# Token-major projection blocks 512 columns wide on two PSUM banks, in a two-layer hybrid encoder

## The chip, the cores and the metric

One core of one Trainium2 chip runs the whole program. The metric is the device time of one execution in microseconds (us). A profiled execution is a separate one; its span runs from the first to the last profiled instruction.

## The reference

Input x is (1, 256, 2048) in float32. After a LayerNorm come two layers, each with an input projection of 6144 columns, an SSM over half of the width (64 groups of 16 channels, 64 states, both directions), differential attention with 8 heads over the other half, and an output projection with a residual and a LayerNorm:

```python
x = layer_norm(x, ln_emb_g, ln_emb_b)
for l in range(DEPTH):                                  # 2
    u, g_ssm, q, k, v, g_attn = split(x @ w_in[l])      # 1024 columns each
    y = u * ssm_d[l] + s5_scan(u, forward) + s5_scan(u, backward)
    y = gelu(y); y = y * sigmoid(y @ w_glu[l] + b_glu[l])
    y_ssm = y * silu(g_ssm)
    o = (softmax(q1 k1') - lam * softmax(q2 k2')) @ v   # 8 heads, q and k rotated
    y_attn = rms_norm(o) * attn_norm_g[l] * (1 - lambda_init) * silu(g_attn)
    x = layer_norm(ALPHA * x + concat(y_ssm, y_attn) @ w_out[l])
```

## The kernel before

All weights are streamed once, in jobs of 512 KB that a list `jobs` (lines 124 to 139) orders for both layers: `load` (143) brings a job into one of four `raw` buffers on SP's DMA queue, six jobs ahead of its use, and `do_split` (155) casts it, two jobs ahead, into a high part `wh` (ScalarE, line 162) and a low part `wl` (VectorE, line 164). A product is three matmuls, high by high, high by low, low by high (`mm3`, 167 to 170). Activations stand in x pairs `xh0`, `xl0` (the first 1024 rows of the contraction) and `xh1`, `xl1`, laid out with the 256 tokens in the free dimension.

A job holds 4 contraction tiles of 128 by 256 columns, so it is 24 matmuls of 256 columns (`sub_step`, 841). Where `tok_major` is false the weights are the stationary operand and the 256 tokens move: q, k, u, both gates, the GLU. Where it is true 128 tokens are stationary and 256 weight columns move: v and the output projection. A `block` (859) is 4 jobs into one PSUM bank of the tag `acc`, which has two banks; blocks alternate between them. The output projection's blocks are 2 jobs for each half of its contraction: first the attention half (line 943, result with the residual in `part_r`), after the GLU the SSM half (976), whose last blocks run token half by token half (988 to 1014) so that the LayerNorm of the first half begins early.

Beside the jobs run helpers ("lanes", 754 to 798): after each job `step` (829) calls `side`, which lets helpers of priority below 2 take a step and gives the others 1.6 us of VectorE cost (`BUDGET`). A helper says with each step what it costs and how many jobs it wants to wait. `ssm_load` (403) brings in B and C and transposes them, `ssm_in` (460) and `ssm_scan` (544) run the states, `ssm_out` (557) makes y by way of DRAM and, in `split_y` (621), its Gelu and its split. `head` (699) is one attention head: scores, softmax, product with v, RMS norm, and, after a further hop, two transposes of `on` into `oT` (746 to 750). `rotary_split` (690) prepares q and k. For the second layer `ssm_load` is started in the last stage of the first (971 to 979): it loads the tables and B there and the rest in the second layer's first jobs.

Instructions get their place on their engine by a list scheduler that works with estimated times; each engine then runs its list in order. `after` (115) keeps an instruction behind a given one of the same engine. `ln_finish` (214) ends a layer; in the last one it cuts the second token half's columns into pieces (`LAST_PIECES`, in units of 128) and stores each with two DMAs from SP (line 240).

Of the kernel before, what the change touches and what calls it, by code (L numbers as in the profile page):

```python
# [20 lines left out]
KT = 4  # L21
# [10 lines left out]
LAST_PIECES = (6,5,5)  # L32
# [7 lines left out]
HEAD_HOPS = (1,1,2,2,2,3)  # L40


@with_exitstack
def kernel(
# [80 lines left out]
    for l in range(DEPTH):  # L125
        for s in range(4):
            jobs += [(l, "in", 0, s), (l, "in", 1, s)]
        order = [2, 3]
        for hp in range(4):
            order += [8 + hp, 12 + hp, 16 + hp]  # L130
        order += list(range(20, 24)) + list(range(4, 8))
        for cb in order:
            jobs += [(l, "in", cb, s) for s in range(4)]
        for cb in range(8):
            jobs += [(l, "out", cb, 2), (l, "out", cb, 3)]
        for cb in range(4):
            jobs += [(l, "glu", cb, 0), (l, "glu", cb, 1)]
        for cb in range(8):
            jobs += [(l, "out", cb, 0), (l, "out", cb, 1)]
    raws, split = {}, {}  # L140
    newest = [None]

    def load(i):
        if i >= len(jobs):
            return
        l, kind, cb, s = jobs[i]
        src = {"in": w_in, "glu": w_glu, "out": w_out}[kind][l]
        raw = T([128, KT, 256], "raw", RAW_BUFS)
        newest[0] = SY.dma_start(
            raw,  # L150
            src[s * KT * 128:(s + 1) * KT * 128, cb * 256:(cb + 1) * 256].rearrange("(k p) c -> p k c", p=128),
# [3 lines left out]
    def do_split(i, wh=None, wl=None, behind=None):  # L155
# [3 lines left out]
        if wh is None:  # L159
            wh = T([128, KT, 256], "wh", SPLIT_AHEAD + 1, F32R)  # L160
            wl = T([128, KT, 256], "wl", SPLIT_AHEAD + 1, F32R)
        A.copy(wh, raw)  # L162
        with after(behind):
            V.tensor_tensor(wl, raw, wh.bitcast(F32), sub)  # L164
        split[i] = (wh, wl)

    def mm3(o, lh, ll, rh, rl, first, last):
        PE.matmul(o, lhsT=lh, rhs=rh, start=first, stop=False, skip_group_check=True)  # L168
        PE.matmul(o, lhsT=lh, rhs=rl, start=False, stop=False, skip_group_check=True)  # L169
        PE.matmul(o, lhsT=ll, rhs=rh, start=False, stop=last, skip_group_check=True)  # L170
# [43 lines left out]
    def ln_finish(r, gt, bt, st, dst, box, ahead):  # L214
# [16 lines left out]
        def norm(i, k0, nk, mv, rstd):  # L231
# [63 lines left out]
    def ssm_tables():  # L295
# [65 lines left out]
        for l in range(2):  # L361
# [3 lines left out]
            else:  # L365
                tt = [T([128, 2, 256], "v", 2) for _ in range(2)] + [T([128, 1, 256], "on")]
# [190 lines left out]
    def ssm_out(l):  # L557
# [74 lines left out]
        for o in range(9):  # L632
# [13 lines left out]
            if o < 8:  # L646
                part(ws[o], z, o, 2, z.C, 1, 0, sub, 1)
                toep(o)
                yield 1.8, 0, 0.5
        load_y()  # L650
        yield 0.0, 2
# [47 lines left out]
    def head(hp, h, q, k, v, oT, neg, gsc):  # L699
# [33 lines left out]
        for i in range(2):  # L733
            for k in range(2):
                PE.matmul(o[:, i, :], lhsT=wT[:, k, i * 128:(i + 1) * 128], rhs=v[:, k, h * 128:(h + 1) * 128],  # L735
                          start=k == 0, stop=k == 1)
        ms = T([128, 2], "ms", 2)
        on = T([128, 2, 128], "on")
# [119 lines left out]

    def block(hi, lo, n=4, tok_major=False):
# [5 lines left out]
    for l in range(DEPTH):  # L865
# [6 lines left out]
        else:  # L872
            l_tab = l_load = Lane(l_load, 1)
# [28 lines left out]
        oT = T([128, 8, 256], "a8", 3)  # L902
        store = {}
        heads, every = [], []
        for hp in range(4):
# [15 lines left out]
            every += [Lane(head(hp, h, store["q"], store["k"], v, oT, neg, gsc), 1 + 0.1 * h) for h in range(2)]  # L921
            heads = every[-2:]
        for b in range(4):
            acc = block(hi, lo)
            if b == 3:
                for a in every:
                    finish(a)
            sg = T([128, 2, 256], "qs" if b == 3 else "sh")
            A.activation(sg, acc, AF.Silu)
            V.tensor_tensor(oT[:, 2 * b:2 * b + 2, :], oT[:, 2 * b:2 * b + 2, :], sg, mult)  # L930
        sgs = T([128, 8, 256], "a8", 3)
        for b in range(4):
            acc = block(hi, lo)
            A.activation(sgs[:, 2 * b:2 * b + 2, :], acc, AF.Silu)

        M = Pair()
        for c in range(4):
            cs = slice(2 * c, 2 * c + 2)
            A.copy(M.h[0][:, cs], oT[:, cs])
            V.tensor_tensor(M.l[0][:, cs], oT[:, cs], M.h[0][:, cs].bitcast(F32), sub)  # L940

        part_r = [T([128, D], tag) for tag in ("xh1", "xl1")]
        for cb in range(8):
            cs = slice(cb * 256, (cb + 1) * 256)
            xr = T([128, 2, 256], "xr", 2)
            SY.dma_start(xr, xres[:, cs].rearrange("(i p) d -> p i d", p=128))
            acc = acc_bank()
            for s in (0, 1):
                sub_step(acc, s, M.hi, M.lo, 0, 7, tok_major=True)
# [21 lines left out]
        if l + 1 < DEPTH:  # L971
            l_load = ssm_load(l + 1)
# [104 lines left out]
```

## Time and profile before

| | us |
|---|---|
| median of 3 runs | 1000.04 (999.7 to 1003.74) |
| profiled execution | 1002.55 |
| its span | 1000.8 |

In the profile PE is TensorE's matmuls, PEld its weight loads, DVE is VectorE, ACT ScalarE, POOL GpSimd, SP the engine whose queue issues the DMAs. Matmuls overlap one another, so a matmul's duration is not what it costs; the distance between starts is. The granted clock of a stretch is the mean share of TensorE's full clock of 2.4 GHz, and 1.2 GHz is its other level. Times of single instructions are from the span's start. The first layer's jobs run to about 505 us, the second's from about 517.

### The profile page before, as it was taken

The numbers are of one execution on the slowest core, as the hardware profiler recorded it, in microseconds if no ns is written. First come the engines' busy times: TensorE is split into PE (matmuls) and PEld (weight loads), VectorE is DVE, ScalarE is ACT, GpSimd is POOL, SyncE is SP. The second block draws the span as 40 slices with busy tenths as digits, with TensorE's granted clock in tenths as the row PEclk, the third lists the DMA queues.
The fourth block names the chain that finished last, engine by engine and source line by source line (L and its number), as shares of the span: only waits on it lengthen the run. The fifth ranks groups of instructions, "written<-read, shape, count | busy, mean of one in ns | idle before, by whom it ended". The sixth has DMA issues, their size and how long they took to land.

```text
span 1000.8 us, 24625 instructions
## 1 busy us (share of the span) xinstructions
PE 955.8 (96%) x10304; PEld 926.8 (93%) x10304; DVE 780.3 (78%) x1353; ACT 576.0 (58%) x950; POOL 71.7 (7%) x103
## 2 busy tenths in 40 slices
PE   2999999999999998999979999999999999999995
PEld 2989988999999998999979989999999999999995
DVE  6875799899887786656588699899899759565676
ACT  2546588565575697545344585555556769843640
POOL 1000130210200000000011030010100100000001
PEclk9999999999999999999989999999999999999998
DMA  9898521545554643779875724555445454576953
GB/s 272 254 256 230 184 81 44 168 149 169 156 183 153 193 145 104 234 228 260 215 231 167 233 68 126 170 169 161 157 150 187 151 168 136 178 237 209 270 173 85
DMA packets 193167, 177.76 MB, mean 178 GB/s; under 512 B 37536, under 2 KB 185760, under 8 KB 193056
## 3 DMA queue, kind: packets, MB, share of 16 engines
q1 hardware_dynamic: 193056, 176.18, 58.7%
q8 instruction: 81, 1.33, 0.6%
q14 instruction: 30, 0.25, 0.1%
HBM read 165.02 MB, written 11.14 MB: 176 GB/s over the span
## 4 chain that ended last, share of the span: by engine, by line
PE 81%; DMA 7%; DVE 6%; ACT 3%; issue 1%; SPq 1%; POOL 0%; POOLq 0%; DVEq 0%; ACTq 0%
PE acc L168 23%; PE acc L169 23%; PE acc L170 23%; DMA raw<-in_w_out_dram 3%; PE ss L596 2%; DVE wl L164 2%; PE ss L501 1%; PE sc L707 1%; PE ss L735 1%; PE tp L473 1%; ACT wh L162 1%; PE tp L577 1%; DVE w L456 1%; DVE H L235 1%; DMA H<-in_x_dram 1%
## 5 line engine op out<-in xcount | busy, mean ns | idle before, releaser
L164 DVE TENSOR_TENSOR wl<-raw,wh 128x1024 fp32r<-128x1024 f32 x266 | 324.9, 1223 | 143.0 <-ACT wh L162 141.8
L162 ACT CAST wh<-raw 128x1024 fp32r<-128x1024 f32 x266 | 278.2, 1050 | 251.0 <-PE acc L169 118.7
L168 PE MATMUL acc<-xh,wh 128*128 128x256 f32 x1280 | 370.9, 290 | 0.8 <-ACT xh L252 0.5
L169 PE MATMUL acc<-xl,wh 128*128 128x256 f32 x1280 | 365.2, 286 | 0.8 <-DVE xl L253 0.7
L170 PE MATMUL acc<-xh,wl 128*128 128x256 f32 x1280 | 364.1, 285 | 1.1 <-DVE wl L164 1.1
L168 PEld LDWEIGHTS acc<-xh,wh 128*128 128x128 f32 x1280 | 245.5, 192 | 6.2 <-ACT xh L252 1.4
L169 PEld LDWEIGHTS acc<-xl,wh 128*128 128x128 f32 x1280 | 245.7, 192 | 2.4 <-DVE xl L253 1.5
L170 PEld LDWEIGHTS acc<-xh,wl 128*128 128x128 f32 x1280 | 245.6, 192 | 2.1 <-DVE wl L164 1.5
L168 PE MATMUL acc<-wh,xh 128*128 128x256 f32 x512 | 146.3, 286 | 0.0
L169 PE MATMUL acc<-wl,xh 128*128 128x256 f32 x512 | 145.4, 284 | 0.0
L170 PE MATMUL acc<-wh,xl 128*128 128x256 f32 x512 | 145.0, 283 | 0.0
L169 PEld LDWEIGHTS acc<-wl,xh 128*128 128x128 f32 x512 | 98.2, 192 | 0.2
L168 PEld LDWEIGHTS acc<-wh,xh 128*128 128x128 f32 x512 | 98.1, 192 | 0.1
L170 PEld LDWEIGHTS acc<-wh,xl 128*128 128x128 f32 x512 | 98.2, 192 | 0.0
L169 PE MATMUL acc<-wl,a 128*128 128x256 f32 x208 | 59.1, 286 | 2.1 <-DVE wl L164 2.1
L168 PE MATMUL acc<-wh,a 128*128 128x256 f32 x208 | 58.7, 284 | 0.0
L170 PE MATMUL acc<-wh,a 128*128 128x256 f32 x208 | 58.5, 283 | 0.0
L551 DVE TENSOR_TENSOR sa<-tab,H 128x256 f32<-128x256 f32 x126 | 53.0, 421 | 2.9 <-ACT H L504 0.7
L458 DVE TENSOR_TENSOR w<-w,x 128x512 f32<-128x512 f32 x64 | 45.6, 712 | 0.8
L169 PEld LDWEIGHTS acc<-wl,a 128*128 128x128 f32 x208 | 39.7, 191 | 3.3 <-DVE wl L164 3.3
L717 ACT ACTIVATE e<-sc,mx 128x256 f32<-128x256 f32 x64 | 29.5, 477 | 21.0 <-DVE mx L711 21.0
L168 PEld LDWEIGHTS acc<-wh,a 128*128 128x128 f32 x208 | 39.7, 191 | 0.4 <-ACT wh L162 0.4
(198 smaller groups left out, 1482.9 us busy)
## 6 DMA issues: line engine op xcount, KB each, us to landing
raw<-in_w_in_dram SPq DMA_DIRECT2D x192, 512.0 KB, 3.8
raw<-in_w_out_dram SPq DMA_DIRECT2D x64, 512.0 KB, 4.6
raw<-in_w_glu_dram SPq DMA_DIRECT2D x16, 512.0 KB, 4.4
xr<-xres SPq DMA_DIRECT2D x16, 256.0 KB, 4.3
xres<-H SPq DMA_DIRECT2D x14, 256.0 KB, 3.4
H<-in_x_dram SPq DMA_DIRECT2D x8, 256.0 KB, 5.9
u_dr<-ub SPq DMA_DIRECT2D x8, 256.0 KB, 3.3
a<-u_dr SPq DMA_DIRECT2D x8, 256.0 KB, 3.8
```

The costliest lines, as they stand in the source:

```text
L162: A.copy(wh, raw)
L164: V.tensor_tensor(wl, raw, wh.bitcast(F32), sub)
L168: PE.matmul(o, lhsT=lh, rhs=rh, start=first, stop=False, skip_group_check=True)
L169: PE.matmul(o, lhsT=lh, rhs=rl, start=False, stop=False, skip_group_check=True)
L170: PE.matmul(o, lhsT=ll, rhs=rh, start=False, stop=last, skip_group_check=True)
L235: last = V.scalar_tensor_tensor(r[:, i, cs], r[:, i, cs], rstd, bt[:, cs], mult, add)
L456: V.tensor_tensor(dst, t.unsqueeze(2).to_broadcast([128, 8, 16, 4]), M[:, m, gs, :].unsqueeze(3).to_broadcast([128, 8, 16, 4]), mult)
L458: V.tensor_tensor(w[:, r], w[:, r], x2, op)
L473: PE.transpose(t[:, pr, :], ws[o][:, ri, 2 * pr:2 * pr + 2].rearrange("p g c j -> p (g c j)"), ident)
L551: V.tensor_tensor(a.rearrange("p v q r g -> p v q (r g)"), lam, h.unsqueeze(1).to_broadcast([128, 2, 16, 8]), mult)
L596: PE.matmul(yps[d][halves[g2], pr, :], lhsT=w[halves[d], ri, g].rearrange("p c j -> p (c j)"), rhs=h[:, ::-1] if d else h, start=ri == 0, ...
L717: A.activation(e[:, m, i, :], sc[:, m, i, :], AF.Exp, bias=mx[:, c:c + 1], accum_out=sm[:, c:c + 1])
```

## The change

Blocks of v, of the attention gate and of the output projection become wide: a job of theirs is 2 contraction tiles by 512 columns, of the same 512 KB, with 128 tokens stationary, and a block fills both `acc` banks, one for each token half. v is done for four heads at a time. The attention half of the output projection is four wide blocks of 4 jobs; of the SSM half three wide blocks in the first layer and two in the second, the rest as before. A head leaves its result in `oh` with tokens in rows; the gate is applied there, and `to_mix` transposes and splits it inside the last SSM-gate block. The residual comes in two tiles per block. k's rotary is finished at once. The Gelu is kept behind the newest weight cast; y's load and split are a helper of their own. In the second layer all of `ssm_load` runs in the first jobs, with its tables' and B's DMAs behind the newest raw load. The last LayerNorm's pieces are 6, 5, 3, 2, and of each pair of output stores the second is issued by ScalarE.

```diff
-LAST_PIECES = (6,5,5)
+LAST_PIECES = (6,5,3,2)
+WIDE = (3, 2)
+Y_HOP = 3
+LATER_HOP = 2
...
+        for n in range(2):
+            order += [("in", 8 + 2 * n), ("inw", 8 + n), ("in", 12 + 2 * n), ("in", 9 + 2 * n), ("in", 13 + 2 * n)]
+        order += [("inw", 10), ("inw", 11)] + [("in", cb) for cb in range(4, 8)]
...
+        return (2, 512) if jobs[i][1] in ("inw", "wide") else (KT, 256)
...
-        A.copy(wh, raw)
+        newest[2] = A.copy(wh, raw).ins
...
-                for j in range(2):
-                    SY.dma_start(dst[2 * i + j][:, cs], r[64 * j:64 * j + 64, i, cs])
+                for j, eng in enumerate((SY, A)):
+                    eng.dma_start(dst[2 * i + j][:, cs], r[64 * j:64 * j + 64, i, cs])
...
-            SY.dma_start(tabs[l], tab_dr)
+            with after(newest[0]):
+                SY.dma_start(tabs[l], tab_dr)
+            yield 0.0, LATER_HOP
...
-            SY.dma_start(nat[64 * ri:64 * ri + 64], src[l].rearrange("d g p c -> g d (p c)"))
-            yield 0.0, 1 + ri
+            with after(newest[0] if l else None):
+                SY.dma_start(nat[64 * ri:64 * ri + 64], src[l].rearrange("d g p c -> g d (p c)"))
+            yield 0.0, 1 + ri * (4 if l else 1)
...
-                A.activation(z.yT[:, cs], z.yT[:, cs], AF.Gelu_apprx_tanh)
+                with after(newest[2]):
+                    A.activation(z.yT[:, cs], z.yT[:, cs], AF.Gelu_apprx_tanh)
...
+    def ssm_y(l):
+        load_y, split_y = ssm[l].y_lane
         load_y()
-        yield 0.0, 2
+        yield 0.0, Y_HOP
         split_y()
...
-        yield 0.0, HEAD_HOPS[4]
-        t = tp_bank([128, 256])
-        for i in range(2):
-            PE.transpose(t[:, i * 128:(i + 1) * 128], on[:, i, :], ident)
-        A.activation(oT[:, 2 * hp + h, :], t, AF.Copy, scale=gsc)
...
+    def wide_block(hi, lo, s0, n):
+
+        accs = [PS([128, 512], "acc", 2) for _ in range(2)]
+        for s in range(s0, s0 + n):
+            def fn(wh, wl):
+                for i in range(2):
+                    ms = slice(128 * i, 128 * i + 128)
+                    for k in range(2):
+                        kt = 2 * s + k
+                        mm3(accs[i], hi(kt)[:, ms], lo(kt)[:, ms], wh[:, k, :], wl[:, k, :],
+                            kt == 2 * s0, kt == 2 * (s0 + n) - 1)
+            step(fn)
+        return accs
...
-            l_tab = l_load = Lane(l_load, 1)
+            l_tab = l_load = Lane(ssm_load(l), 1)
...
+            if hp % 2 == 0:
+                accs = wide_block(hi, lo, 0, 8)
+                finish(rq)
+                v = T([128, 2, 512], "v")
+                for i in range(2):
+                    A.copy(v[:, i], accs[i])
...
-            rk.one()
-            acc = block(hi, lo, tok_major=True)
-            v = T([128, 2, 256], "v", 2)
-            A.copy(v, acc)
             finish(rk)
...
+        def to_mix(b):
+
+            for c in range(2 * b, 2 * b + 2):
+                t = tp_bank([128, 2, 256])
+                for n in range(2):
+                    for i in range(2):
+                        with after(newest[3]):
+                            PE.transpose(t[:, n, 128 * i:128 * i + 128],
+                                         oh[:, i, (2 * c + n) * 128:(2 * c + n + 1) * 128], ident)
+                cs = slice(2 * c, 2 * c + 2)
+                A.activation(M.h[0][:, cs], t, AF.Copy, scale=gsc)
+                V.scalar_tensor_tensor(M.l[0][:, cs], t, gsc, M.h[0][:, cs].bitcast(F32), mult, sub)
+
+        for b in range(2):
+            accs = wide_block(hi, lo, 0, 8)
+            for a in every[4 * b:4 * b + 4]:
+                finish(a)
+            cs = slice(512 * b, 512 * b + 512)
+            for i in range(2):
+                sg = T([128, 512], "qs" if i else "sh")
+                A.activation(sg, accs[i], AF.Silu)
+                V.tensor_tensor(oh[:, i, cs], oh[:, i, cs], sg, mult)
...
+            for n in range(4):
+                sub_step(acc, n, hi, lo, 0, 15)
+                if b == 3 and n in (1, 2):
+                    to_mix(n - 1)
...
+        for cb in range(4):
+            cs = slice(cb * 512, (cb + 1) * 512)
+            xrs = []
             for i in range(2):
-                V.scalar_tensor_tensor(part_r[i][:, cs], xr[:, i], ALPHA, acc[:, i, :], mult, add)
-        finish(l_out)
+                xrs.append(T([128, 512], "xr", 2))
+                SY.dma_start(xrs[i], xres[128 * i:128 * i + 128, cs])
+            accs = wide_block(M.hi, M.lo, 0, 4)
+            for i in range(2):
+                V.scalar_tensor_tensor(part_r[i][:, cs], xrs[i], ALPHA, accs[i], mult, add)
+        finish(l_y)
...
-        if l + 1 < DEPTH:
-            l_load = ssm_load(l + 1)
...
+        for cb in range(WIDE[l]):
+            accs = wide_block(M.hi, M.lo, 4, 4)
+            cs = slice(cb * 512, (cb + 1) * 512)
+            for i in range(2):
+                V.tensor_tensor(r[:, i, cs], part_r[i][:, cs], accs[i], add)
+                for c in range(2):
+                    ln_stats(r, i, 2 * cb + c, st)
+        for cb in range(2 * WIDE[l], late[0]):
```

## Rows read from the trace of the kernel before

**Rows 1.** Page, part 1: busy us, share of the span, instructions, by engine
```profile
PE 955.8 (96%) x10304; PEld 926.8 (93%) x10304; DVE 780.3 (78%) x1353; ACT 576.0 (58%) x950; POOL 71.7 (7%) x103
```

**Rows 2.** Page, part 4: the chain that ended last, by engine
```profile
PE 81%; DMA 7%; DVE 6%; ACT 3%; issue 1%; SPq 1%; POOL 0%; POOLq 0%; DVEq 0%; ACTq 0%
```

**Rows 3.** Stretches: length; busy PE, PEld, DVE, ACT, POOL; granted clock, DMA share, GB/s
```profile
380.00:392.00 12.00, 9.15 (x203) 8.69 (x200) 8.40 (x14) 10.44 (x19) 0.00 (x0) 0.87 0.37 112
470.00:505.00 35.00, 33.11 (x264) 31.74 (x263) 21.86 (x35) 13.42 (x13) 0.00 (x0) 1.00 0.89 219
505.00:530.00 25.00, 20.15 (x150) 19.21 (x149) 21.75 (x39) 8.59 (x14) 2.54 (x4) 0.86 0.69 216
614.00:770.00 156.00, 156.00 (x1334) 153.86 (x1334) 141.66 (x290) 87.78 (x175) 11.32 (x18) 1.00 0.53 163
877.00:922.00 45.00, 45.00 (x378) 45.00 (x377) 27.32 (x33) 16.45 (x16) 0.00 (x0) 1.00 0.75 232
```

**Rows 4.** Timeline of TensorE: start, us, engine, line, op, out<-in, shapes, count
```profile
172.79 1.05 PE L735 MATMUL ss<-v,wT 128*128 128x128 f32 x8
...
454.83 0.28 PE L168 MATMUL acc<-bh,wh 128*128 128x256 f32 x1
...
455.89 0.28 PE L168 MATMUL acc<-bh,wh 128*128 128x256 f32 x1
...
896.53 0.28 PE L170 MATMUL acc<-wh,xl 128*128 128x256 f32 x1
...
899.41 0.28 PE L170 MATMUL acc<-wh,xl 128*128 128x256 f32 x1
```

**Rows 5.** Timeline of ScalarE and VectorE at a block's end in the output projection
```profile
896.85 1.05 ACT L162 CAST wh<-raw 128x1024 fp32r<-128x1024 f32 x1 [1.83 <-PE acc L170]
896.85 0.42 DVE L951 SCALAR_TENSOR_TENSOR xh<-xr,acc 128x256 f32<-128x256 f32 x1 [0.58 <-PE acc L170]
...
897.93 1.23 DVE L164 TENSOR_TENSOR wl<-raw,wh 128x1024 fp32r<-128x1024 f32 x1 [0.32 <-ACT wh L162]
```

**Rows 6.** Groups by line: engine op names shapes count, busy us, mean ns, idle before
```profile
L201 DVE BATCH_NORM_STATS2 st<-H 128x6 f32<-128x256 f32 x48 | 18.1, 416 | 8.2 <-DMA H<-in_x_dram 8.0
...
L229 DVE SCALAR_TENSOR_TENSOR H<-H,mv 128x512 f32<-128x512 f32 x18 | 13.4, 746 | 0.1
...
L934 ACT ACTIVATE a<-acc 128x512 f32<-128x512 f32 x8 | 4.8, 596 | 0.1
```

**Rows 7.** Timeline of ScalarE, then TensorE, first layer's SSM outputs
```profile
383.75 1.28 ACT L626 ACT_TABLE_LOAD   x1 [1.33 <-DMA a<-y_dr]
...
385.44 0.28 PE L170 MATMUL acc<-xh,wl 128*128 128x256 f32 x1
388.56 0.50 PE L596 MATMUL ss<-bh,w 64*64 64x64 f32 x8 [2.85 <-ACT ub L607]
```

**Rows 8.** Page, part 6: DMA issues: count, KB each, median us to landing
```profile
xr<-xres SPq DMA_DIRECT2D x16, 256.0 KB, 4.3
```

**Rows 9.** Chain before the boundary (start, us, what); timeline of VectorE, TensorE at it
```profile
468.71 13.70 DMA raw<-in_w_out_dram
...
519.76 0.48 DVE L235 SCALAR_TENSOR_TENSOR H<-H,rstd 128x256 f32<-128x256 f32 x1 [0.47 <-POOL rstd L224]
...
521.02 1.94 PE L446 MATMUL tp<-cst,a 128*128 128x128 f32 x8 [4.31 <-DMA a<-in_ssm_c_re_dram]
522.75 1.06 PE L248 MATMUL ss<-cst,H 128*128 128x128 f32 x4
```

**Rows 10.** Timeline of ScalarE, second layer: last Gelu, first sigmoid's table
```profile
866.67 1.15 ACT L626 ACTIVATE a<-a 128x512 f32<-128x512 f32 x2
...
926.49 1.28 ACT L967 ACT_TABLE_LOAD   x1
```

**Rows 11.** Timeline of VectorE and of SP's queue at the end
```profile
994.47 1.68 DVE L235 SCALAR_TENSOR_TENSOR H<-H,rstd 128x640 f32<-128x640 f32 x2
...
995.88 1.88 SPq L240 DMA_DIRECT2D out_dram<-H  x3
```

More of the change, by code (lines that the diff above doesn't have):

```diff
@@ L127, with shape_of @@
             jobs += [(l, "in", 0, s), (l, "in", 1, s)]
[L128 to L135, printed above, removed]
+        order = [("in", 2), ("in", 3)]
+        for n in range(2):
+            order += [("in", 8 + 2 * n), ("inw", 8 + n), ("in", 12 + 2 * n), ("in", 9 + 2 * n), ("in", 13 + 2 * n)]
+        order += [("inw", 10), ("inw", 11)] + [("in", cb) for cb in range(4, 8)]
+        for kind, cb in order:
+            jobs += [(l, kind, cb, s) for s in range(4 if kind == "in" else 8)]
+        for cb in range(4):
+            jobs += [(l, "wide", cb, s) for s in range(4, 8)]
         for cb in range(4):
             jobs += [(l, "glu", cb, 0), (l, "glu", cb, 1)]
-        for cb in range(8):
+        for cb in range(WIDE[l]):
+            jobs += [(l, "wide", cb, s) for s in range(4)]
+        for cb in range(2 * WIDE[l], 8):
             jobs += [(l, "out", cb, 0), (l, "out", cb, 1)]
     raws, split = {}, {}
-    newest = [None]
+    newest = [None] * 4
+    def shape_of(i):
+        return (2, 512) if jobs[i][1] in ("inw", "wide") else (KT, 256)
     def load(i):
@@ L146, in load @@
         l, kind, cb, s = jobs[i]
-        src = {"in": w_in, "glu": w_glu, "out": w_out}[kind][l]
-        raw = T([128, KT, 256], "raw", RAW_BUFS)
+        src = {"in": w_in, "inw": w_in, "glu": w_glu, "out": w_out, "wide": w_out}[kind][l]
+        k, n = shape_of(i)
+        raw = T([128, k, n], "raw", RAW_BUFS)
         newest[0] = SY.dma_start(
             raw,
-            src[s * KT * 128:(s + 1) * KT * 128, cb * 256:(cb + 1) * 256].rearrange("(k p) c -> p k c", p=128),
+            src[s * k * 128:(s + 1) * k * 128, cb * n:(cb + 1) * n].rearrange("(k p) c -> p k c", p=128),
         ).ins
@@ L159, in do_split @@
         if wh is None:
-            wh = T([128, KT, 256], "wh", SPLIT_AHEAD + 1, F32R)
-            wl = T([128, KT, 256], "wl", SPLIT_AHEAD + 1, F32R)
-        A.copy(wh, raw)
+            wh = T([128, *shape_of(i)], "wh", SPLIT_AHEAD + 1, F32R)
+            wl = T([128, *shape_of(i)], "wl", SPLIT_AHEAD + 1, F32R)
+        newest[2] = A.copy(wh, raw).ins
         with after(behind):
-            V.tensor_tensor(wl, raw, wh.bitcast(F32), sub)
+            newest[1] = V.tensor_tensor(wl, raw, wh.bitcast(F32), sub).ins
         split[i] = (wh, wl)
@@ L169, in mm3 @@
         PE.matmul(o, lhsT=lh, rhs=rl, start=False, stop=False, skip_group_check=True)
-        PE.matmul(o, lhsT=ll, rhs=rh, start=False, stop=last, skip_group_check=True)
+        newest[3] = PE.matmul(o, lhsT=ll, rhs=rh, start=False, stop=last, skip_group_check=True).ins
     class Pair:
@@ L365, in ssm_tables @@
             else:
-                tt = [T([128, 2, 256], "v", 2) for _ in range(2)] + [T([128, 1, 256], "on")]
+                tv_ = T([128, 4, 256], "v")
+                tt = [tv_[:, 0:2], tv_[:, 2:4], T([128, 1, 256], "on")]
                 rows = [tt[q // 2][:, q % 2, :] for q in range(5)]
@@ L901 @@
         l_scan = Lane(ssm_scan(l), 5, after=[l_in])
-        oT = T([128, 8, 256], "a8", 3)
+        oh = T([128, 2, 1024], "a8", 3)
         store = {}
         heads, every = [], []
+        v = None
         for hp in range(4):
@@ L920 @@
                 l_out = Lane(ssm_out(l), 4, after=[l_scan])
-            every += [Lane(head(hp, h, store["q"], store["k"], v, oT, neg, gsc), 1 + 0.1 * h) for h in range(2)]
+                l_y = Lane(ssm_y(l), 4, after=[l_out])
+            every += [Lane(head(hp, h, store["q"], store["k"], v, oh, neg, gsc), 1 + 0.1 * h) for h in range(2)]
             heads = every[-2:]
[L923 to L930, printed above, removed]
+        M = Pair()
@@ L970 @@
             V.tensor_tensor(M.l[1][:, cs], sg, M.h[1][:, cs].bitcast(F32), sub)
-        if l + 1 < DEPTH:
-            l_load = ssm_load(l + 1)
         places = [("bh", "c8")] if l + 1 < DEPTH else [("bh", "c8"), ("xh0", "xl0")]
         late = range(7 - len(places), 8)
-        for cb in range(late[0]):
-            if l + 1 < DEPTH and cb in (0, 2):
-                with after(newest[0]):
-                    next(l_load)
+        for cb in range(WIDE[l]):
+            accs = wide_block(M.hi, M.lo, 4, 4)
[5 more added lines that the diff above has]
+        for cb in range(2 * WIDE[l], late[0]):
             cs = slice(cb * 256, (cb + 1) * 256)
```

22 lines of the change are left out of this document (6 added, 16 removed).

## Prediction, made before the changed kernel was run

> **What bounds the kernel now.** First the page's busy times: TensorE is busy 96% of the span, VectorE 78%, ScalarE 58% [rows 1]. Then the chain that ended last: 81% of it is TensorE, 7% DMA, 6% VectorE [rows 2], so what shortens TensorE's queue shortens the kernel unless another wait takes its place. Then the stretches [rows 3]: in the heads' stage of the second layer (614 to 770 us) and in the first half of its output projection (877 to 922) TensorE has no idle time, at the full clock of 2.4 GHz. Beside it VectorE is 91% busy in the former (141.66 of 156) and 61% in the latter, so the heads' stage has little room on VectorE. Three places are not like that: TensorE lost 1.9 us in pieces at 470 to 505, 2.9 us at 380 to 392, and 4.9 us where the second layer begins (505 to 530). In the last two the mean granted clock is 0.87 and 0.86, so part of each ran at 1.2 GHz.
>
> Next what one matmul costs. Its shown duration (0.28 us, [rows 4]) is a latency; the spacing counts. Between two matmuls of one line that lie 24 apart pass 899.41 - 896.53 = 2.88 us, 120 ns each for 256 columns [rows 4]. A column per cycle of 2.4 GHz would be 106.7 ns, so 13.3 ns lie above that. In the GLU, with other tiles as operands, nine take 455.89 - 454.83 = 1.06 us, 118 ns. A 128-column weight load with a 128-column matmul passes in (1.05 - 0.27) / 7 = 111 ns [rows 4].
>
> **The wide matmuls (first term).** Per layer v (4 blocks of 4 jobs), the attention gate (4 of 4) and the attention half of the output projection (8 of 2) have 16 jobs each; the SSM half gets 12 wide jobs in the first layer and 8 in the second. A job is 24 matmuls of 256 columns. That is 48 + 48 + 20 = 116 jobs, 2784 matmuls, 334.1 us at 120 ns. They become 1392 of 512 columns, with half as many weight loads. No row has 512 columns. Ends: a column per cycle and nothing else, 213.3 ns; or all of the 120 ns per column, 240 ns. I take the 13.3 ns as a cost per instruction, 226.7 ns, because the GLU's rows lose 2 ns with no column less, so the excess isn't a column rate; and because a load that passes in 111 ns lies wholly under 213. So 1392 x (240 - 226.7) = **18.5 us less** (ends 0 and 37.1). Bytes, jobs and casts stay as they are; the two casts per job (1.05 us on ScalarE, 1.23 on VectorE, [rows 5]) still fit in a job of 12 x 226.7 ns = 2.72 us. Where VectorE is 91% busy, only v shortens TensorE, by 16 jobs x 0.16 = 2.6 us a layer; VectorE's idle 14 us there take that.
>
> The Trainium skill (TensorE: Matmul & The Clock Gate, Back-to-back issue gap) gives columns / 2.4 + 2.5 ns, that is 109 ns for 256 and 216 for 512. The trace differs at 256: 120. By the page alone a pair would save 2.5 ns, 3.5 us in all; the page's 216 against the trace's 240 would be 33 us.
>
> **Both banks in one block (second term).** Today a block fills one bank while the other is emptied, so a whole block hides the emptying. A wide block takes both; the next needs its first bank at once. Within its last job of 2.72 us token half 0 ends its six matmuls first: the sixth starts at 1.13 and ends some 0.39 later (0.28 and 107 ns for 256 more columns), at 1.52. VectorE's cast of the coming weights is in the way: the job before ends with the matmul at 896.53, so this one starts at 896.65; ScalarE's half of the cast starts at 896.85 and VectorE's at 897.93 [rows 5], 1.28 to 2.51 in the job. A 512-column eviction is not in the trace for these lines; the nearest are 0.75 us on VectorE and 0.60 on ScalarE [rows 6], against 0.42 for 256 [rows 5]. Behind the cast the bank is free at 3.26, 0.54 late; ahead of the cast it is free in time. I take half, 0.27, for the 13 blocks that VectorE empties (8 attention half, 5 SSM half): 3.5. In the SSM half two statistics of 0.42 [rows 6] stand between the two evictions: 3.26 + 0.83 + 0.75 = 4.84 against a need at 3.26 + 1.36 = 4.62, 0.2 x 5 = 1.0. The 4 gate blocks are emptied by Silu, with a table load of 1.28 [rows 7] ahead of it where Exp ran before: 1.56 + 1.28 + 0.60 = 3.44, 0.7 late, in three or four of them: 2.4. The 4 v blocks: 1.56 + 0.60 is in time unless ScalarE is in the heads' exponentials, 0.2 each: 0.8. Together **7.7 us more**. The ends are 0 (each eviction is listed first) and 40 (rival C).
>
> What waits behind these: the next weight casts on VectorE move by at most 1.6 us, and their job is two jobs (5.4 us) away; raw loads on SP follow the casts and are four buffers ahead. The residual tiles now take both xr buffers in one block, so SP's two xr loads wait for the evictions, with raw loads queued behind; xr lands in 4.3 us [rows 8] and is needed four jobs (10.9 us) later, so this costs nothing while the evictions are under 6 us late.
>
> **Heads gated by rows (no term).** The 16 transposes of `on` per layer move from the heads to two groups of 8 in the last SSM-gate block, same number and cost. ScalarE loses 8 evictions per layer, and the mix is split straight from PSUM. The block's last jobs (two, 5.4 us) cover the four splits; uncovered they would cost the first output block at most 4 x 0.75 = 3 us per layer.
>
> **Gelu pinned (third term).** At 383.75 ScalarE began the first Gelu's table load after waiting for half of y from DRAM, with the copies for the SSM's outputs queued behind it. TensorE waited for those from 385.44 to 388.56 [rows 7]: 3.0 us beyond one spacing, and then 12 x (1 - 0.87) = 1.6 us at the lower clock [rows 3]. Behind the newest cast, and three jobs after the load, the Gelu no longer stands ahead of the copies: **4.6 us less**. If a Gelu still waits there, 0.
>
> **B and C in the second layer (fourth term).** The tables and B (three DMAs) leave the end of the first layer, where raw weights took 13.70 us to land [rows 9] and TensorE lost 1.9. Four C loads and four small ones shift behind them. On SP the three are pinned behind a raw load each, among the stores of x. At the boundary the C transposes waited 4.31 us for their DMA and held the LayerNorm transposes until 522.75; VectorE had the second token half normalised at 519.76 + 0.48 = 520.24 [rows 9], so 2.4 us are free. But 32 transposes (111 ns each by the nearest row, 3.5 us) then all fall into full TensorE time, of which some 8 (0.9) do so today: 2.6 back. Net 2.4 + 1.9 - 2.6 = **1.7 us less**; ends 4.3 less, and 4.6 more if a transpose is again put ahead of its data. The SSM chain of the second layer starts some 8 jobs (23 us) later. Its last Gelu ran at 866.67 and the first GLU sigmoid's table load at 926.49 [rows 10]: those 60 us hide the delay, which otherwise would cost what goes beyond them.
>
> **The tail (fifth term).** The second half of each output store goes by ScalarE's queue, so the last two issues no longer follow one another: SP's last three took 1.88 us, 0.6 each [rows 11]: **0.6 us less** (0 to 1). The extra cut of the last piece leaves VectorE's work there, whose last two scalings took 1.68 [rows 11], as long.
>
> **Sum.** -18.5 + 7.7 - 4.6 - 1.7 - 0.6 = -17.7. The profiled execution, 1002.55 us (span 1000.8 and 1.75 around it), would be 984.9; it lies 2.5 above the median of the runs shown, and against that median, 1000.04, the forecast is **982.3 us**, by itself 974 to 991.
>
> **Rivals.** A: the whole excess over a column per cycle goes, 213.3 ns: another 18.6 less, 963.7. For it: the load would be hidden wholly. Against it: no row is below 118 at 256.
> B: 240 ns, the cost is per column: 18.5 back, 1000.8. For it: 120 holds in nearly all stages, with either operand stationary. Against it: the GLU's 118.
> C, the slower side: the banks become the bound. VectorE serves the cast and then a helper's slice, up to the 1.6 us that a step is given, before it empties the bank: free at 1.28 + 1.23 + 1.6 + 0.75 = 4.86, 2.1 late, 13 times; ScalarE is late by 1.5, 8 times: 40 us instead of 7.7, 1014.6. It decides the sign from 1.45 us per wide block on (982.3 - 7.7 + 21 x 1.45 = 1005). For it: VectorE at 91% among the heads. Against it: 61% where eight of the blocks end, and there the eviction begins the moment the last matmul has ended [rows 5].
> D: the stops lower the clock. The stop of 3.1 us was followed by 1.6 us lost at 1.2 GHz [rows 3, 7]; 21 such would be 34 us, 1016. Stops that sum to 1.9 at 470 to 505 left it at 1.00 [rows 3], and mine are 0.7. The Trainium skill (TensorE: Matmul & The Clock Gate, A second HAM failure mode: psum-queue depth-cycling) says that cycling through banks at 512 columns makes the clock swing; no run here shows it.
> E: the moved waits give nothing, the third term 0 and the fourth +4.6: 993.2.
>
> **How the numbers follow.** Forecast 0.55, A 0.12, B 0.13, C 0.08, D 0.03, E 0.09. About 0.5% (5 us) is what a measurement of this kernel can tell from no change. Faster by more: 0.55 + 0.12 + 0.05 of E = 0.72. Within: 0.04 of E, 0.11 of B, 0.02 of C = 0.17. Slower: 0.02 of B, 0.06 of C, 0.03 = 0.11. The range leaves out about 0.1 on each side: 966 (most of A lies below it) to 1002.
>
> **What would show it.** Spacing of 512-column matmuls: 227 ns right, near 213 A, near 240 B. TensorE's idle time at each wide block's end and its releaser: under 0.7 us right, above 1.4 C. Granted clock in the output projection: 1.00 right. No wait of 2.9 us for a copy near the end of the first layer's SSM outputs, none of 4.3 for C. The forecast is wrong if the spacing is off by more than 7 ns (10 us), or if another order of the queues opens stops that no row shows.

## The result, and the profile after

| | before | after |
|---|---|---|
| median, us | 999.99 | 1050.35 (1048.91 to 1055.5) |
| span of the profiled execution, us | 1000.8 | 1048.0 |
| granted clock, mean of the span | 0.991 | 0.958 |

The ratio is 1.0504, 95% interval 1.046 to 1.0547. The forecast was 982.3 with a range that ended at 1002: wrong in sign, and none of the five rivals is the reason. What the prediction gave last as a sign of being wrong is what happened: another order of the queues opened stops that no row shows.

The busy times of the page of after come first, against [rows 1]:

```profile
PE 976.7 (93%) x8912; PEld 878.9 (84%) x8912; DVE 781.1 (75%) x1329; ACT 573.3 (55%) x933; POOL 72.0 (7%) x103
```

TensorE has 1392 matmuls fewer, as the change says, and is busy longer. VectorE and ScalarE do what they did. So matmuls went slower somewhere. The stretches of after, with the columns of [rows 3], show where:

```profile
358.00:397.00 39.00, 31.56 (x474) 29.75 (x475) 17.67 (x29) 21.01 (x42) 0.00 (x0) 0.52 0.22 63
470.00:505.00 35.00, 34.63 (x225) 31.39 (x224) 21.60 (x26) 19.45 (x26) 0.00 (x0) 1.00 0.75 241
505.00:530.00 25.00, 24.25 (x138) 20.88 (x138) 19.00 (x28) 9.66 (x10) 0.78 (x1) 1.00 0.65 211
614.00:770.00 156.00, 152.80 (x1728) 136.52 (x1727) 139.52 (x260) 94.85 (x172) 21.32 (x25) 1.00 0.45 136
867.00:899.00 32.00, 22.30 (x357) 21.31 (x354) 12.61 (x21) 15.79 (x30) 0.00 (x0) 0.52 0.26 71
921.00:967.00 46.00, 44.59 (x195) 35.76 (x193) 27.02 (x27) 17.77 (x19) 0.00 (x0) 1.00 0.66 214
```

The attention half of the second layer's output projection, four wide blocks (921 to 967), is near the forecast: full clock, idle for 1.4 of 46 us. The loss is in 358 to 397 and 867 to 899, inside the SSM gate's stage of each layer: clock 0.52 and 0.52 (1.2 GHz nearly throughout), DMA share 0.22 and 0.26, one weight cast in the two together (17 in before). The same times in before:

```profile
358.00:397.00 39.00, 35.46 (x761) 33.59 (x754) 30.57 (x47) 34.93 (x63) 0.00 (x0) 0.96 0.39 117
867.00:899.00 32.00, 32.00 (x269) 32.00 (x268) 22.93 (x27) 18.01 (x22) 0.00 (x0) 1.00 0.68 216
```

From the last attention-gate Silu to the last eviction of the attention half, a layer took 116.8 and 112.3 us before, 139.6 and 137.7 after: 48 us of the 50 lost. ScalarE's timeline of after begins with the last cast of weights for a long time:

```profile
353.51 1.04 ACT L173 CAST wh<-raw 128x1024 fp32r<-128x1024 f32 x1
...
372.36 1.15 ACT L642 ACTIVATE a<-a 128x512 f32<-128x512 f32 x2
...
388.36 1.14 ACT L645 CAST bh<-a 128x512 fp32r<-128x512 f32 x2 [2.12 <-PE ss L611]
389.52 0.37 ACT L622 COPY ub<-ss 128x256 f32<-128x256 f32 x1
389.91 1.28 ACT L988 ACT_TABLE_LOAD   x1
391.20 1.09 ACT L988 ACTIVATE a<-acc 128x512 f32<-128x512 f32 x2
396.93 1.05 ACT L173 CAST wh<-raw 128x1024 fp32r<-128x1024 f32 x1 [4.64 <-PE acc L180]
```

L988 is the SSM gate's Silu into `sgs`. Before it ran block by block, at 334.6, 346.3, 364.1 and 392.6; here the first two run together at 391. Until then both `acc` banks are full, no further gate matmul can start, no weights are cast, and TensorE is left with the SSM's small matmuls, in groups with waits for copies between them. TensorE of after:

```profile
358.18 0.45 PE L611 MATMUL ss<-bh,w 64*64 64x64 f32 x8 [1.40 <-ACT ub L622]
...
379.39 0.69 PE L611 MATMUL ss<-bh,w 64*64 64x64 f32 x8 [1.32 <-ACT ub L622]
...
391.85 0.58 PE L179 MATMUL acc<-xh,wh 128*128 128x256 f32 x1 [3.32 <-ACT a L988]
```

In SP's queue, y's load for the Gelu (L633) stands at 367.89, long ahead of that Silu:

```profile
365.27 0.37 SPq L628 DMA_DIRECT2D y_dr<-ub  x1
367.89 0.37 SPq L633 DMA_DIRECT2D a<-y_dr  x1
379.82 11.20 SPq L628 DMA_DIRECT2D y_dr<-ub  x2
```

y and `sgs` share the tag `a8` of three buffers with `z.U`, the SSM's input, and `oh`. The program hands buffers out in the order in which it asks for them. In after it asks for y first, and y takes the free one; `sgs` must then wait for the buffer of `z.U`, which the SSM outputs read to their end (the last L616 matmul starts at 388.2). Before, it asked for `sgs` first, and y, loaded at 380.06, took the buffer that the mix had just left.

### The profile page after: what moved, and what is told of

It reads as the page before. It is cut to its first block, busy times and chain, and to the rows that moved or that the text cites. A ratio compares the mean times of both kernels' runs of the same rounds, so it can differ in the third digit from the quotient of the medians.

```text
span 1048.0 us, 21813 instructions
## 1 busy us (share of the span) xinstructions
PE 976.7 (93%) x8912; PEld 878.9 (84%) x8912; DVE 781.1 (75%) x1329; ACT 573.3 (55%) x933; POOL 72.0 (7%) x103
## 4 chain that ended last, share of the span: by engine, by line
PE 80%; ACT 5%; DVE 5%; DMA 4%; issue 3%; POOL 2%; SPq 1%; POOLq 0%; DVEq 0%; ACTq 0%
PE acc L179 22%; PE acc L180 21%; PE acc L181 21%; PE ss L611 4%; ACT wh L173 2%; PE ss L516 2%; PE sc L727 2%; PE tp L488 2%; POOL ms L761 1%; DVE wl L175 1%; PE ss L755 1%; DMA raw<-in_w_in_dram 1%; PE tp L592 1%; PE ss L616 1%; PE tp L497 1%
## 5 line engine op out<-in xcount | busy, mean ns | idle before, releaser
L179 PE MATMUL acc<-xh,wh 128*128 128x256 f32 x1024 | 296.6, 291 | 11.1 <-ACT a L988 6.6
L180 PE MATMUL acc<-xl,wh 128*128 128x256 f32 x1024 | 295.1, 288 | 1.2 <-DVE xl L264 1.0
L181 PE MATMUL acc<-xh,wl 128*128 128x256 f32 x1024 | 294.0, 287 | 0.1
L181 PEld LDWEIGHTS acc<-xh,wl 128*128 128x128 f32 x1024 | 198.5, 194 | 1.2 <-DVE wl L175 0.3
L180 PE MATMUL acc<-wl,xh 128*128 128x512 f32 x384 | 153.0, 399 | 0.0
L181 PE MATMUL acc<-wh,xl 128*128 128x512 f32 x384 | 151.2, 394 | 0.0
L179 PE MATMUL acc<-wh,xh 128*128 128x512 f32 x384 | 144.9, 398 | 2.2 <-DVE xh L999 2.2
L611 PE MATMUL ss<-bh,w 64*64 64x64 f32 x1024 | 51.3, 274 | 10.8 <-ACT ub L622 10.5
L611 PEld LDWEIGHTS ss<-bh,w 64*64 64x64 f32 x1024 | 48.1, 173 | 13.5 <-ACT ub L622 11.6
L179 PE MATMUL acc<-wh,a 128*128 128x512 f32 (+1 forms) x128 | 43.5, 352 | 1.9 <-DVE H L1026 1.5
L181 PE MATMUL acc<-wh,a 128*128 128x512 f32 (+1 forms) x128 | 44.7, 349 | 0.0
```

The source lines that it names most:

```text
L181: newest[3] = PE.matmul(o, lhsT=ll, rhs=rh, start=False, stop=last, skip_group_check=True).ins
L611: PE.matmul(yps[d][halves[g2], pr, :], lhsT=w[halves[d], ri, g].rearrange("p c j -> p (c j)"), rhs=h[:, ::-1] if d else h, start=ri == 0, ...
```

## The experiments

All ratios are to the kernel before, run beside each experiment on the same chip (its medians there: 1002.08 to 1002.78), with the 95% interval behind them. Each diff is against the kernel that its experiment starts from.

**The buffer's order.** Three runs. e1 is after, with y's helper created behind the first Silu into `sgs`:

```diff
             if hp == 0:
                 l_out = Lane(ssm_out(l), 4, after=[l_scan])
-                l_y = Lane(ssm_y(l), 4, after=[l_out])
...
             A.activation(sgs[:, 2 * b:2 * b + 2, :], acc, AF.Silu)
+            if b == 0:
+                l_y = Lane(ssm_y(l), 4, after=[l_out])
```

> The changed kernel with one edit: the helper that loads y is only started once the first SSM-gate block has written its Silu into sgs, so sgs gets the third buffer of tag a8 and y's load waits for the release of U. Theory (buffer order): the 36 us in which TensorE gets no job of the input projection while both acc banks wait for sgs go, with the stretches at 1.2 GHz of 37.5 and 30.7 us; from the last gate to the last eviction of the attention half the layers return from 139.6 and 137.7 us to about 115 each: 1050 - 25 - 23 = 1002 us. Rival 1 (wide blocks holding both banks starve TensorE) and rival 2 (the pinned Gelu holds ScalarE): nothing of this depends on the buffer, 1050.

Measured 1011.67, ratio 1.0107 (1.0077 to 1.0138): some 39 us back. The two stretches of e1:

```profile
358.00:397.00 39.00, 35.49 (x566) 32.83 (x562) 26.40 (x38) 29.36 (x48) 0.00 (x0) 0.99 0.48 144
867.00:899.00 32.00, 30.50 (x177) 26.33 (x177) 20.66 (x22) 19.15 (x25) 0.00 (x0) 1.00 0.64 196
```

e2 starts from after again and asks why the order turned round. The change finishes k's rotary at once; before, its second half was a helper's step, whose cost was drawn from the others' budget. Uncharged, the first layer's SSM outputs begin at job 79 instead of 88, and y is asked for at job 84, just ahead of the first Silu into `sgs`, instead of 93. e2 draws the cost from the budget again:

```diff
             finish(rk)
+            clock[1] -= 3.6
```

> The changed kernel with one edit: k's rotary, which is finished at once, is charged to the helpers' budget (3.6 us per pair of heads), so the SSM helpers come as late in the list as before the change and y's load again follows the first write of sgs. Theory (buffer order, and the uncharged rotary as what reversed it): about 1002 us, the stop gone as with the other order. Rival (the order of the two is set by something else, the wide blocks or the pinned Gelu): 1050.

1015.5, ratio 1.0159 (1.0128 to 1.0189): the same stop gone by another way. The first Silu into `sgs` runs at 334.0 us again, y's load at 388.0. The 4 us to e1 are met again under e15. e9 makes the same reversal in the kernel before, with nothing wide:

```diff
-            rk.one()
+            finish(rk)
             acc = block(hi, lo, tok_major=True)
             v = T([128, 2, 256], "v", 2)
             A.copy(v, acc)
-            finish(rk)
```

> The kernel before with one line moved: the second half of k's rotary is written out right after its first half, as the change does, so that its cost is not charged to the helpers' budget. Nothing is wide, Gelu, B and C stay. In the program's order y's load then stands ahead of the first Silu into sgs in both layers (it stood behind it). If the third a8 buffer going to y instead of sgs is what costs the changed kernel its time, this one line costs the kernel before about as much as e1 gave back to the changed kernel (1050.4 - 1011.7 = 38.7): 1035 to 1045, no weight cast on ScalarE for some 35 us at the end of the gate blocks in both layers, TensorE at 1.2 GHz for 30 us and more in each. If the loss needs the wide blocks, the row gating or the wide Silu (rival), it stays within 5 us of the time before, 1000 to 1007.

1027.25, ratio 1.0245 (1.0216 to 1.0274). Its ScalarE has the same gap: the last weight cast at 361.89, the first Silu into `sgs` (L933) at 384.83. TensorE was at 1.2 GHz for 23.9 us; the stretch of e9, columns as above:

```profile
358.00:392.00 34.00, 25.65 (x416) 24.43 (x414) 16.46 (x28) 21.17 (x38) 0.00 (x0) 0.65 0.28 87
```

So one line that belongs to no term of the sum costs 25 us. That is less than the 39 of e1 and than e9 expected; in the second layer the low clock lasted only 3.4 us. Why the reversal costs more beside the rest of the change wasn't tried by itself.

**Two terms alone.** e4 is before with the Gelu kept behind the newest cast; e5 is before with the second layer's tables, B and C loaded in its own first jobs, as the change does.

> The kernel before with the Gelu pin alone. The prediction's third term: the wait of 3.0 us for a copy near 388 us and the 1.6 us at 1.2 GHz behind it go: 995.4 us. Rival: the Gelu, one cast later, stands ahead of other work that TensorE waits for: 1000 or above.

> The kernel before with the second layer's tables, B and C loaded in its first jobs, and nothing else of the change. The prediction's fourth term: 998.3 us (1.7 less; ends 4.3 less and 4.6 more). Rival: the LayerNorm sets the boundary anyway, and the 32 transposes in full TensorE time cost 2.6: 1002.

e4: 1004.05, ratio 1.0014 (0.9991 to 1.0038). TensorE still stops for 3.1 us, and ScalarE's timeline of e4 still has the Gelu's table load ahead of the copy for the SSM outputs:

```profile
383.09 1.05 ACT L162 CAST wh<-raw 128x1024 fp32r<-128x1024 f32 x1
385.47 1.28 ACT L627 ACT_TABLE_LOAD   x1 [1.33 <-DMA a<-y_dr]
386.76 1.15 ACT L627 ACTIVATE a<-a 128x512 f32<-128x512 f32 x2
387.82 2.02 ACT L639 COPY bh<-H 128x1024 f32<-128x1024 f32 x1
```

The newest cast was ahead of the Gelu anyway: the pin changes no order. e5: 1010.58, ratio 1.0099 (1.0077 to 1.012), 8.5 us slower. From the last sigmoid to the last eviction the end of the first layer gains 4.4 us (47.1 for 51.4). TensorE's wait at the boundary is no shorter and has another releaser (4.88 us for LayerNorm, where before waited 4.31 for C). From the last attention-gate Silu to the first eviction of the output projection, the second layer's SSM-gate stage grows from 72.3 to 81.7 us. ScalarE of e5 there:

```profile
879.13 1.28 ACT L630 ACT_TABLE_LOAD   x1
884.23 1.15 ACT L630 ACTIVATE a<-a 128x512 f32<-128x512 f32 x2 [3.81 <-DMA a<-y_dr]
885.29 1.03 ACT L163 CAST wh<-raw 128x1024 fp32r<-128x1024 f32 x1
```

The later SSM chain brings the Gelu late, ScalarE waits 3.81 us for y with a weight cast queued behind, and TensorE waits 2.90 for that cast at 886.37. TensorE's waits in that stage sum to 4.9 us, where before had none, and 6.8 us at 1.2 GHz begin at 886.3.

**The banks.** e6 is e1 with the tables, B and C placed as before; e7 writes VectorE's half of the weight cast in a wide output block's last job, and the raw load with it, out behind the two evictions; e11 pins it there (the same in the SSM half):

```diff
             for i in range(2):
-                V.scalar_tensor_tensor(part_r[i][:, cs], xrs[i], ALPHA, accs[i], mult, add)
-            for h in held:
-                h()
+                last = V.scalar_tensor_tensor(part_r[i][:, cs], xrs[i], ALPHA, accs[i], mult, add)
+            with after(last.ins):
+                for h in held:
+                    h()
```

> e1 (the changed kernel with y's buffer taken behind sgs) with the tables, B and C of the second layer loaded where the kernel before loads them. If the price of that placement is its own (8.5 us measured alone) and adds, e1's 1011.7 becomes 1003; if it is worth nothing beside the wide blocks, 1011. The rest of the change (wide blocks -18.5 by the measured spacing, bank stops +6.9, Gelu 0) would give 1002.1 - 11.6 = 990.5 if nothing else were in the way.

> e6 with one order changed on VectorE: in the last job of each wide output block the subtraction for the coming weights (and the raw load behind it) is written out behind the two evictions. If the 0.53 us at each of the 13 blocks is the cast standing ahead of the eviction, the 13 stops go and the time is e6's less 6.9 us. If the bank is late for another reason (the eviction's own length, a helper's slice), the stops stay and the time is e6's.

> e7 (whole change, y's buffer behind sgs, tables, B and C as before) with the cast pinned behind the evictions as in e10. 13 stops of 0.53 us: 1014.0 - 6.9 = 1007 if the cast holds the bank; 1014 if not.

e6 1015.52, ratio 1.013 (1.0092 to 1.0167); e7 1014.01, 1.012 (1.0092 to 1.0148); e11 1011.68, 1.0089 (1.0063 to 1.0116). In e7 VectorE's order had not moved, and twelve stops stayed (starts 0.76 us apart instead of 0.227; at the thirteenth block stands a wait for B). VectorE of e7:

```profile
407.70 1.22 DVE L178 TENSOR_TENSOR wl<-raw,wh 128x1024 fp32r<-128x1024 f32 x1 [1.11 <-ACT wh L173]
408.84 0.68 DVE L1007 SCALAR_TENSOR_TENSOR xh<-xr,acc 128x512 f32<-128x512 f32 x1
409.44 0.68 DVE L1007 SCALAR_TENSOR_TENSOR xl<-xr,acc 128x512 f32<-128x512 f32 x1
```

and of e11, where the first eviction begins when its matmuls end and the cast comes third:

```profile
409.37 0.69 DVE L1007 SCALAR_TENSOR_TENSOR xh<-xr,acc 128x512 f32<-128x512 f32 x1 [1.57 <-PE acc L187]
410.50 0.69 DVE L1007 SCALAR_TENSOR_TENSOR xl<-xr,acc 128x512 f32<-128x512 f32 x1 [0.45 <-PE acc L187]
411.11 2.36 DVE L178 TENSOR_TENSOR wl<-raw,wh 128x1024 fp32r<-128x1024 f32 x2
```

The next block's first matmul follows at 411.66, one spacing behind the last, and no stop of 0.53 us is left in the attention halves. The cast is the cause of the stops. Only some 3 us of the 6.9 that they sum to came back, though; where the rest went wasn't followed. e6's missing gain has its own row in its trace, as in that of e8 below: B's transposes ahead of their data (a wait of 5 us from 489 on, and 6.8 us at 1.2 GHz).

**The output projection alone.** e8 is before with only the output projection wide and e7's writing order; e10 adds the pin; e12 adds to e10 that B's transposes stay behind the first layer's last matmul; e13 is e11 with the same.

```diff
-            for c in range(4):
-                PE.transpose(t[:, c, :], natv[:, :, 4 * q + c], ident)
+            with after(newest[3] if l else None):
+                for c in range(4):
+                    PE.transpose(t[:, c, :], natv[:, :, 4 * q + c], ident)
```

> The kernel before with only the output projection wide (attention half in both layers, three and two blocks of the SSM half), its banks emptied ahead of the cast; v, gates, heads, Gelu, B and C as before, so y's load stands where it stood. 52 jobs of 12 matmuls, each 240 - 226.7 ns shorter by the prediction's first term: 8.3 us less, 994. If the spacing of 213 ns were within reach without the stops: 16.6 less. If stops of the banks or the clock take it: 1000 or more.

> e8 (the kernel before with the output projection wide) with the weight cast that falls into a block's end pinned behind the block's second eviction, since writing it out behind them did not move it in e8 and e7: the cast still began at 407.70 us, 1.14 ahead of the eviction. If the cast is what holds the bank, the ten stops of 0.53 us go (5.3 us; 13 stops, 6.9 us, if those of the last SSM-half blocks count) and the time is 1009.3 - 6 = 1003, with the 5.4 us wait for B's DMA at 487 us and its low clock still there. If the eviction itself is late, the stops stay and the time is 1009.

> e10 with B's transposes of the second layer kept behind the last matmul of the first layer, so that none stands ahead of its DMA at 487 us. If that wait (5.4 us in e8, and 6.8 us at 1.2 GHz behind it) is what the wide SSM half costs in the first layer, this is e10 less 8 us: 995, under the kernel before by the 8.3 us of 52 jobs at 227 ns for 512 columns. If the 16 transposes then stand in full TensorE time and the boundary's wait for LayerNorm takes the rest, 1000 to 1003.

> e11 with B's transposes behind the last matmul of the first layer as in e12: 1007 - 8 = 999. The v stops (1.70 twice), the wait for the mix's split (2.8 in the first layer) and for a gate bank (1.74) are left in it; without them it would be at the 990 that the prediction's first term gives. If it stays over 1003, wide v and gates cost more than their 10.2 us bring.

| | us | ratio |
|---|---|---|
| e8 | 1009.28 | 1.006 (1.0038 to 1.0082) |
| e10 | 999.19 | 0.9958 (0.9935 to 0.998) |
| e12 | 1001.28 | 0.9977 (0.9954 to 1.0) |
| e13 | 1007.99 | 1.0056 (1.0029 to 1.0082) |

TensorE of e8 has this between two wide blocks of the first layer's SSM half:

```profile
492.06 1.33 PE L435 MATMUL tp<-cst,a 128*128 128x128 f32 x5 [4.98 <-DMA a<-in_ssm_b_im_dram]
```

The scheduler put these transposes there, some 8 us earlier than in the kernel before (500.74), ahead of their DMA; the clock is at 1.2 GHz for 6.8 us from 489.2 on. In e10 the wait at that place is 1.2 us. So e10's 10 us against e8 are made up of two things that its trace doesn't show any more: the twelve bank stops of e8 (6.4 us), and most of this wait with its low clock. e10 is the first that is faster than before, by 4 us of the 8.3 that its 52 wide jobs save by their spacing. Holding B's transposes back (e12) brings nothing on top, since LayerNorm then sets the boundary (4.8 us for DVE's H at 516), and late evictions at the end of the SSM half stop TensorE for 3.1 us (0.5 in e10); e13 gains 3 us on e11. The 995 expected for e12 was wrong by that.

**What was left.** e13 is still 8 us over e12 by the ratios, though wide v and gate should bring 10. e14 is e13 with v narrow and k's rotary as before; e15 is e13 with k's rotary charged, as in e2; e16 is e10 with the Gelu eight jobs behind y's load, so that it does stand behind the last copy for the SSM outputs.

> e13 (whole change with y's buffer behind sgs, B and C as before, casts pinned, B's transposes late) with v in 256-column blocks again and k's rotary finished behind v's block, charged, as in the kernel before; the attention gate stays wide and the heads gated by rows. e12 has neither wide v nor wide gate (ratio 0.998), e13 both (1.0056). If v and the order around k are what costs, this comes back to e12's 1000 less the gate's 32 jobs x 0.16 = 5.1: 995 to 1000. If the gate and the row gating cost, it stays at 1006 to 1010.

> e13 with k's rotary charged to the helpers' budget (3.6 us for each head pair), so that the SSM outputs begin at job 88 and 217, as in the kernel before, instead of 79 and 208. If their earlier start among the heads is what e13 still loses (its heads' stage of the second layer took 224.2 us against 216.5), this is 1008 - 5 = 1003 or less; if the waits of v's emptying (1.70 us twice), of the mix's split and the gates' banks are it, 1006 to 1010.

> e10 (only the output projection wide, casts pinned) with the Gelu eight jobs behind y's load and pinned behind the newest cast: now it stands behind the last copy for the SSM outputs in ScalarE's order, which the pin alone and a hop of three jobs did not bring. If the 3.2 us wait at 386 us is the Gelu's table load ahead of that copy, it goes, with up to 1.7 us of low clock: 999 - 3 to 5 = 994 to 996. If another copy or the y transfer is late, 999.

e14: 1000.13, ratio 0.9978 (0.9962 to 0.9994). e15: 1000.88, 0.9978 (0.9951 to 1.0004). e16: 1001.84, 1.0008 (0.9988 to 1.0028). So the uncharged rotary, which moves every helper behind it forward, cost 7 us in e13 by itself, apart from the buffer. This doesn't hold everywhere: e2, with the same charge, is 4 us slower than e1. In e2 the product of y and `sgs` (L1014 below) stops TensorE in both layers (4.8 us at 400 and 3.6 at 889), in e15 in the first alone. e16 removes the 3.2 us wait at 386 and gets two others: 2.5 us at 414.6, where VectorE does the product of y and `sgs` ahead of a bank's eviction, and 2.9 us at 873.9 in the second layer. That product stops e14 and e15 too (4.3 and 3.5 us from start to start); VectorE of e15:

```profile
401.16 2.29 DVE L1014 TENSOR_TENSOR a<-a,a 128x2048 f32<-128x2048 f32 x1
403.37 0.68 DVE L1009 SCALAR_TENSOR_TENSOR xh<-xr,acc 128x512 f32<-128x512 f32 x1
```

e17 and e18 are e15 and e14 with the product pinned behind the attention half's last eviction:

```diff
-        V.tensor_tensor(z.yT, sgs, z.yT, mult)
+        with after(last.ins):
+            V.tensor_tensor(z.yT, sgs, z.yT, mult)
```

> e15 with one more instruction pinned on VectorE: the product of y and sgs (128x2048, 2.29 us), which stood ahead of the first block's evictions in the output projection of the first layer (evictions at 403.37 and 403.96 us, TensorE stopped 3.5 us from 400.72), goes behind the last eviction of the attention half. If that is the stop, it goes with the 3.4 us of low clock behind it: 1000.9 - 3.3 - 1.7 = 996; if another VectorE instruction takes its place, 1001.

> The same pin in e14 (v narrow), where the first block's stop was 4.26 us at 400 us with 6.8 us of low clock behind it: 1000.1 - 4 - 3.4 = 993. Beside e17 it says what wide v is worth once nothing else differs around it: if wide v brings the 5.1 us of 32 jobs x 0.16, e17 is the faster by 2 or more after its v stops (1.7 twice); if the stops take it all, they are equal or e18 is ahead.

e17: **995.71, ratio 0.9916 (0.9891 to 0.9941)**, faster than both kernels. e18: 994.97, 0.9925 (0.9903 to 0.9946). Between the two, wide v is worth nothing that can be told.

## Why the prediction was wrong, point by point

**Wide matmuls (-18.5).** The spacing was right. TensorE of after:

```profile
924.56 0.39 PE L181 MATMUL acc<-wh,xl 128*128 128x512 f32 x1
924.78 0.39 PE L179 MATMUL acc<-wh,xh 128*128 128x512 f32 x1
925.01 0.39 PE L180 MATMUL acc<-wl,xh 128*128 128x512 f32 x1
925.24 0.39 PE L181 MATMUL acc<-wh,xl 128*128 128x512 f32 x1
925.46 0.39 PE L179 MATMUL acc<-wh,xh 128*128 128x512 f32 x1
```

The spacing is 226 to 235 ns, median 227, in the four blocks from 921 to 967; rivals A (213) and B (240) are out. The Trainium skill (TensorE: Matmul & The Clock Gate, Back-to-back issue gap) gives 216 by its formula, for an isolated gap, and 131 as a sustained value for 512 columns; the measured 227 decides. What failed is that the term was taken to be gained in full. v's share, 32 jobs x 0.16 = 5.1 us, doesn't show (e17 against e18); its own stops in e17 are 1.4 us twice.

**Both banks (+7.7).** The mechanism was right, and so was its full size of 0.54 us; the half that the text took was not. It was 0.53 at all 13 blocks: 6.9, not 3.5. The 0.2 for v was off by more at two of its four blocks. There, in after, ScalarE serves a cast and a head's squares first, so that v's copies begin at 227.83 and TensorE starts 1.43 us late, once in each layer:

```profile
226.18 1.04 ACT L173 CAST wh<-raw 128x1024 fp32r<-128x1024 f32 x1 [1.29 <-PE acc L181]
227.13 0.36 ACT L760 ACTIVATE a<-ss,rc 128x128 f32<-128x128 f32 x1
...
227.83 1.07 ACT L946 COPY v<-acc 128x512 f32<-128x512 f32 x2
```

The attention gate's Silu, 0.7 late in three or four blocks by the text, stopped TensorE for 0.8 at one (324 us) and for no more than 0.1 at the other three. The SSM half's 0.2 for the second bank is under 0.1. So the term came to about 10.6 us in after. Rival C's mechanism, other work of VectorE ahead of a bank's emptying, happened once in each of e14 to e16, by one instruction of 2.29 us, not 13 times.

**Heads gated by rows, and k's rotary beside them (no term).** The step that lost the case is k's rotary, which the change finishes at once in the same loop and which the prediction left at nothing without a reason. It priced the 16 transposes and the splits, but not what a step that is no longer a helper's does to the others: no budget is drawn for it, the SSM outputs begin nine jobs earlier, and y asks for its `a8` buffer before `sgs` does. The order of these two requests was never followed, though both are in the code. It cost some 39 us in the changed kernel (e1), of the 68 between forecast and measurement, and 25 in the kernel before (e9). The gating by rows took no part in e9. In e1 the splits were not covered either: TensorE waited 2.5 us for them. That this is near the 3 us given as the uncovered price is chance, since the reason was ScalarE standing 2.53 us for y, with the Gelu at its head.

**Gelu pinned (-4.6).** The step said that behind the newest cast the Gelu "no longer stands ahead of the copies". It still did (e4). Where it was really moved (e16), the wait came back in two other places.

**B and C (-1.7).** Up to the last attention-gate Silu of the second layer the term held: e5's trace is 1.5 us ahead there (806.4 for 807.9). The step that failed is "those 60 us hide the delay": it compared the last Gelu with the first sigmoid. The delay was paid earlier, where ScalarE waits for y ahead of a weight cast (e5: 8.5 us instead of -1.7, beyond the term's end of +4.6). With wide blocks the placement's price doesn't simply add: e6, with B and C as before, is no faster than e1.

**The tail (-0.6).** From the last eviction to the end before took 14.3 us and after 14.1: 0.2.

**Rival D.** Small stops did not lower the clock: 0.53 us at each of four blocks, clock 1.00 from 921 to 967. The swing of the Trainium skill (TensorE: Matmul & The Clock Gate, A second HAM failure mode: psum-queue depth-cycling) isn't seen in these blocks. But the clock did fall, by another cause: 37.5 and 30.7 us at 1.2 GHz, in stretches where TensorE ran little but SSM matmuls between waits. How much of the 48 us there is the low clock's and how much the waits' wasn't separated.

Repaired, the change brings 8.4 us by the ratio (e17; 5.9 to 10.9), of the 18.5. The stops that e17's trace still shows from 160 to 508 us, in the first layer, sum to 12.7 us, and v's in the second layer is 1.6; those of before in the same stretch sum to 7.6 (each taken as the distance of two starts less the usual one, where it is over 0.5 us). This accounts for some 6 or 7 of the 10 that are missing; the rest stays open.

## What to carry to other kernels

A step that moves from a helper into the main line moves every helper behind it. Before such a change, follow the order in which the tiles of one tag are asked for, and who holds the buffer that the loser must wait for. An order written out in the source need not be the order on the engine (e7): look for it in the timeline, and pin the cast behind the eviction where a block takes every bank (e11). A late step's margin ends at the first queue in which it stands ahead of something else, not at its last reader (e5).

## What the runs showed of the hardware

In after, TensorE's granted clock was 0.50 (1.2 GHz) from 358.9 to 396.4 us, where it ran the SSM's 64x64 matmuls in short groups between waits for copies. In the kernel before, the same matmuls stood among gate matmuls, and from 340 to 380 us the clock was 1.00. So, while the gate's matmuls were held up, those that could still run ran at the lower clock. A matmul of 512 columns was shown at 0.39 us, of 256 at 0.28, while their spacings were 227 and 120 ns.
